# One layer of a diffusion backbone: order of the transposed pieces, a key load kept, and five buffers in two sizes

## The chip, the cores and the metric

The kernel runs on 1 core of one Trainium2 chip. The metric is the device time of one execution in microseconds (us); lower is better. All arithmetic of the layer is on the core; the host only supplies two rotary tables.

## The reference, cut to what matters

One trunk layer over 2048 latent tokens and 256 context tokens, width 1024. A combined projection feeds two attention mixers whose queries are the 2048 latent tokens and whose keys are all 2304 tokens; both results are gated, projected, merged and normalised. What bears on the change is the pair of attentions and how the first one's key is made:

```python
k_mla = concatenate([k_nope, broadcast_to(k_r, ...)])      # 8 heads, 64 + 32 columns; k_r is one for all heads
s = einsum('bhqd,bhkd->bhqk', q, k) * scale
o_a = einsum('bhqk,bhkd->bhqd', softmax(s), v)             # 8 heads

s1, s2 = (q1 k1, q2 k2) * scale                            # 4 heads, 64 columns each
p = softmax(s1) - lam * softmax(s2)
o_d = einsum('bhqk,bhkd->bhqd', p, v)
```

The first is called MLA below (kind 0 in the code), the second differential attention (kind 1).

## The kernel before, in words

Three stages follow each other: projections (to about 945 us), attention (to about 2530 us), and the output stage. Values that must be exact to fp32 are kept as a high and a low part, and a product is two or three matmuls.

**Attention.** Work comes in units of 256 queries of one head, two tiles of 128 queries each. There are 64 MLA units (8 heads of 8) and 32 differential ones (4 heads of 8); the order repeats two MLA units and one differential unit, 32 times, with a differential unit ahead. For each tile `softmax_tile` (L673) makes scores on TensorE in three PSUM groups (L682), VectorE takes each out with a running minimum (L683), ScalarE applies the exponential (L696). A differential tile does that twice, and VectorE combines the two (L795).

**`transposed` (L702)** turns a tile of 128 queries by 2304 keys around for the second product. The keys are 18 blocks of 128, in two halves of nine. For each half (e = 0, 1) ScalarE casts blocks to fp16 as a high part (L708), GpSimd subtracts to get the low part (L709, VectorE for some of the last units), and one transposing DMA on SyncE's queue (L710) moves both, turned, into `pts`. The buffer that holds the split, `hl`, comes from a pool of 4 equal buffers. A differential tile does so with 9 + 9 blocks. An MLA tile leaves 4 blocks of its first half out (5 + 9, `NCB` = 5): those four go through TensorE's transpose into the one PSUM buffer `px` (L715), from which ScalarE writes the high part (L717) and VectorE the low part (L718). In the source these four come after both casts.

**The second product** (`mla_av`, `diff_av`, L723 to L757) reads `pts`, has four tiles of `pt` (two units' worth) and runs on TensorE among the scores. A filler on TensorE (L627, gate projections, `pf`) is strewn between.

**Loads.** `load_k` (L799) fetches a head's keys when its first unit comes: three groups of 1024, 768 and 512 keys, each with its own buffer. For MLA, rows 0 to 63 (`kn`) are the head's own, rows 64 to 95 (`kr`) the rotary rows, which are the same for all heads. Both are loaded for each head; after the third unit the loads are issued on ScalarE's queue. MLA heads change seven times, the first at about 1098 us.

**Order.** Source order gives priorities; a planner works out each engine's fixed order when the kernel is built, putting a later instruction ahead where an earlier one is not yet ready by its plan. Every engine then works in that order.

Of the kernel before, what the change touches and what calls it, by code (L numbers as in the profile page):

```python
# [10 lines left out]
F32R = mybir.dt.float32r  # L11
F16 = mybir.dt.float16
I32 = mybir.dt.int32
AF = mybir.ActivationFunctionType
ALU = mybir.AluOpType
# [3 lines left out]
P = 128  # L19
# [44 lines left out]
def layer_kernel(ctx: ExitStack, tc: tile.TileContext, x, c, ctxt, c_ctx, w_mod, b_mod, w_in,  # L64
# [3 lines left out]
    pe, dve, act, pool, sp = nc.tensor, nc.vector, nc.scalar, nc.gpsimd, nc.sync  # L68
# [9 lines left out]
    def dram(name, shape, dt):  # L78
        return dr.tile(shape, dt, tag=name, name=name)
# [7 lines left out]
    kr_s = dram("kr", [32, 2, NT], F32)  # L87
# [502 lines left out]
    with ExitStack() as st:  # L590
        kp, qp_, vp = {}, {}, {}
# [11 lines left out]
        p16 = st.enter_context(tc.tile_pool(name="c16", bufs=4))  # L603
# [12 lines left out]
        def ldma(o, i):  # L616
            lq[0].dma_start(o.bitcast(F32) if o.dtype == F32R else o, i.bitcast(F32) if i.dtype == F32R else i)
# [81 lines left out]
        def new_pts():  # L699
            return [ptp.tile([P, 9, 2, 2, P], F16, tag="pt", name="pt") for _ in range(2)]  # L700

        def transposed(pts, i, s, shared, ncb):  # L702


            for e, n in enumerate((ncb, 9)):
                hl = p16.tile([P, 9, 2, P], F16, tag="hl", name="hl")[:, :n]
                se = s[:, e * 1152:e * 1152 + n * P].rearrange("p (k q) -> p k q", q=P)
                act.copy(hl[:, :, 0], se)  # L708
                (dve if shared and e else pool).tensor_tensor(hl[:, :, 1], se, hl[:, :, 0], op=ALU.subtract)  # L709
                sp.dma_start_transpose(pts[e][:, :n, :, i, :].rearrange("p k l q -> p (k l) q"),  # L710
                                       hl.rearrange("p k l q -> p (k l q)"))
            for k0 in range(ncb, 9, 4):
                px = ps_x.tile([P, 4, P], F32, tag="px", name="px")
                for t in range(4):
                    pe.transpose(px[:, t, :], s[:, (k0 + t) * P:(k0 + t + 1) * P], ident)  # L715
                hi, lo = (pts[0][:, k0:k0 + 4, l, i, :] for l in range(2))
                act.copy(hi, px)  # L717
                dve.tensor_tensor(lo, px, hi, op=ALU.subtract)  # L718

        def pt_part(pts, kt, l):  # L720
            return pts[kt // 9][:, kt % 9, l].rearrange("p i q -> p (i q)")
# [49 lines left out]
        def mla_soft(h, u, qt, ks, pts):  # L771
            for i in range(2):
                qs = qt[0:96, :, i * P:(i + 1) * P]
                k_hi, k_lo = (lambda k: k[0:96, 0, :]), (lambda k: k[0:96, 1, :])
                s = softmax_tile([(qs[:, 0, :], k_hi), (qs[:, 0, :], k_lo), (qs[:, 1, :], k_hi)], ks, MLA_SCALE, LN_PSC,
                                 zs[u][:, i, h:h + 1])
                transposed(pts, i, s, n_ >= len(units) - 2, NCB)
                yield

        def diff_soft(h, u, qt, ks, pts):  # L780
            for i in range(2):
                def scores(m, shift, zsum):
                    qs = qt[:, m, :, i * P:(i + 1) * P]
                    km = (lambda k: k[:, m, :])
                    return softmax_tile([(qs[:, 0, :], km), (qs[:, 1, :], km)], ks, DIFF_SCALE, shift, zsum)


                za = zs[u][:, i, H + h:H + h + 1]
                sa = scores(0, lamc[:, 2:3], za)
                yield  # L790
                w = sm.tile([P, 3], F32, tag="w", name="w")
                sb = scores(1, None, w[:, 0:1])
                dve.reciprocal(w[:, 1:2], w[:, 0:1])
                dve.tensor_scalar(w[:, 2:3], za, w[:, 1:2], lamc[:, 0:1], op0=ALU.mult, op1=ALU.mult)
                dve.scalar_tensor_tensor(sa, sb, w[:, 2:3], sa, op0=ALU.mult, op1=ALU.add)  # L795
                transposed(pts, i, sa, n_ >= len(units) - 3, 9)
                yield

        def load_k(kind, h):  # L799
            ks = []  # L800
            for g, (k0, nk) in enumerate(GS):
                k = kp[kind].tile([P, 2, nk], F32R, tag=f"k{kind}{g}", name=f"k{kind}{g}")
                cs = slice(k0, k0 + nk)
                if kind == 0:
                    ldma(k[0:64], kn_s[h // 2][(h % 2) * 64:(h % 2) * 64 + 64, :, cs])
                    ldma(k[64:96], kr_s[:, :, cs])
                else:
                    ldma(k, dk_s[h][:, :, :, cs].rearrange("l d m n -> (l d) m n"))
                ks.append(k)
            return ks  # L810
# [31 lines left out]
        for n_ in range(len(units) + LAG):  # L842
# [3 lines left out]
            if n_ < len(units):  # L846
                kind, h, u = units[n_]
                if u == 0:
                    ks_[kind] = load_k(kind, h)
                if n_ + 1 < len(units):  # L850
                    qs_.append(load_q(*units[n_ + 1]))
                pts = new_pts()
                soft = (mla_soft if kind == 0 else diff_soft)(h, u, qs_.pop(0), ks_[kind], pts)
            parts = (2 if kind == 0 else 4)
            g = None
            if len(pend) == LAG or (soft is None and pend):
                g = pend.pop(0)(parts)
# [21 lines left out]
    with ExitStack() as st:  # L879
# [20 lines left out]
        with ExitStack() as s1_:  # L900
# [70 lines left out]
            for b in range(8):  # L971
                cs = slice(b * 256, (b + 1) * 256)
# [119 lines left out]
```

## Time and profile before

| | |
|---|---|
| median of 3 runs | 2961.67 us (2951.07 to 2964.77) |
| the profiled execution | 2959.4 us |
| its span, first to last instruction | 2957.3 us |
| busy share of the span | PE 93%, PEld 75%, DVE 60%, ACT 49%, POOL 51% |
| granted TensorE clock, mean | 0.974 |

PE is TensorE's matmuls, PEld its weight loads, DVE VectorE, ACT ScalarE, POOL GpSimd, SP SyncE. An engine's busy time counts execution, not waiting. In the listed waits, "A <- B: total, times, longest" says that A stood idle until B was done. L708 is line 708 of the kernel.

### The profile page before, as it was taken

The page shows a single profiled execution, that of the slowest core. Times are in us where ns is not written, and L with a number is a line of the kernel's source. Part 1 is how long each engine was busy: PE and PEld are TensorE (multiplying, and loading weights), DVE is VectorE, ACT ScalarE, POOL GpSimd, SP SyncE. Part 2 cuts the span into 40 slices and gives each one's busy share as a digit, 9 for nine tenths or more (in the row PEclk, how much of TensorE's full clock was granted, in tenths as well). Part 3 has the DMA queues.
Part 4 walks back from the last instruction along what each step waited for, and adds up shares of the span by engine and source line. Part 5 has one row for each costly group of instructions (what it writes and reads, how often), then busy time and mean ns, then how long its engine had stood idle before and what let it go on. Part 6 is the DMA issues. An engine that isn't in the chain of part 4 may idle for free. (4 is left out here: it accounts for less than half of the span.)

```text
span 2957.3 us, 44828 instructions
## 1 busy us (share of the span) xinstructions
PE 2743.9 (93%) x16049; PEld 2205.0 (75%) x16049; DVE 1789.1 (60%) x3663; ACT 1446.6 (49%) x1885; POOL 1518.7 (51%) x1018
## 2 busy tenths in 40 slices
PE   7999999999999999989999999899899978889998
PEld 5888888879777777767767677677666656789886
DVE  4476310033656777767777777667667778675454
ACT  3333222233324767767766677666676667322110
POOL 2443222232445657658556586565576545464344
PEclk9999999999999999999999999999999989899999
DMA  8467533354566999999999999999999999877542
GB/s 261 124 193 219 165 103 90 97 165 129 147 199 163 194 175 210 187 219 195 176 198 228 213 204 191 196 174 184 195 185 178 198 181 166 232 207 221 178 146 82
DMA packets 1138914, 529.99 MB, mean 179 GB/s; under 512 B 818858, under 2 KB 1090944, under 8 KB 1138692
## 3 DMA queue, kind: packets, MB, share of 16 engines
q1 hardware_dynamic: 1014984, 421.65, 65.0%
q10 hardware_dynamic: 123708, 105.49, 15.1%
q8 instruction: 126, 2.06, 0.3%
q14 instruction: 96, 0.79, 0.1%
HBM read 219.96 MB, written 114.10 MB: 113 GB/s over the span
## 5 line engine op out<-in xcount | busy, mean ns | idle before, releaser
L709 POOL TENSOR_TENSOR hl<-s,hl 128x1152 f16<-128x1152 f32 (+1 forms) x378 | 790.9, 2110 | 468.4 <-ACT hl L708 424.2
L682 PE MATMUL ps<-k,q 96*128 96x512 f32 (+3 forms) x3200 | 822.7, 390 | 44.0 <-DVE s L683 41.2
L682 PEld LDWEIGHTS ps<-k,q 96*128 96x128 f32 (+1 forms) x3200 | 545.1, 192 | 164.7 <-DVE s L683 62.3
L696 ACT ACTIVATE s<-s,z 128x2304 f32<-128x2304 f32 x256 | 567.5, 2217 | 71.6 <-DVE z L689 34.3
L708 ACT CAST hl<-s 128x1152 f16<-128x1152 f32 (+1 forms) x384 | 375.9, 1007 | 345.5 <-DMA pt<-hl 184.5
L683 DVE TENSOR_SCALAR_CACHE_REDUCE s<-ps,z 128x768 f32<-128x768 f32 (+1 forms) x512 | 449.9, 880 | 126.1 <-PE ps L682 107.5
L683 DVE TENSOR_SCALAR_CACHE_REDUCE s<-ps 128x1024 f32<-128x1024 f32 x256 | 312.2, 1219 | 110.6 <-PE ps L682 94.3
L114 PE MATMUL pp<-hT,w 128*128 128x512 f32 (+1 forms) x896 | 347.4, 390 | 9.4 <-DVE qa L337 6.9
L115 PE MATMUL pp<-hT,w 128*128 128x512 f32 (+1 forms) x896 | 348.4, 390 | 0.3 <-DVE hT L272 0.3
L110 POOL TENSOR_TENSOR w<-raw,w 128x512 fp32r<-128x512 f32 (+1 forms) x126 | 163.9, 1307 | 359.7 <-ACT w L107 343.3
L116 PE MATMUL pp<-hT,w 128*128 128x512 f32 (+1 forms) x896 | 346.5, 388 | 0.0
L732 PE MATMUL po<-pt,vd 128*128 128x256 f16 x1728 | 242.4, 280 | 33.1 <-DMA pt<-hl 31.3
L732 PEld LDWEIGHTS <-vd 128*128 128x128 f16 x1728 | 157.8, 100 | 105.9 <-issue 71.8
L114 PEld LDWEIGHTS pp<-hT,w 128*128 128x128 f32 x896 | 169.0, 189 | 47.1 <-DVE qa L337 4.5
L115 PEld LDWEIGHTS pp<-hT,w 128*128 128x128 f32 x896 | 169.6, 189 | 36.4 <-POOL hT L272 0.6
L116 PEld LDWEIGHTS pp<-hT,w 128*128 128x128 f32 x896 | 169.2, 189 | 36.0
L795 DVE SCALAR_TENSOR_TENSOR s<-s,w 128x2304 f32<-128x2304 f32 x64 | 187.1, 2923 | 0.2
L745 PE MATMUL po<-pt,va 128*128 128x256 f16 x1152 | 168.2, 284 | 14.2 <-DMA pt<-hl 14.1
L1026 PE MATMUL pz<-wz,yt 128*128 128x512 f32 x768 | 179.6, 396 | 0.8 <-DVE z L1029 0.8
L1026 PEld LDWEIGHTS pz<-wz,yt 128*128 128x128 f32 x768 | 144.3, 188 | 35.8 <-DVE z L1029 1.3
L718 DVE TENSOR_TENSOR pt<-px,pt 128x512 f16<-128x512 f32 x128 | 87.9, 687 | 128.1 <-ACT pt L717 125.0
L745 PEld LDWEIGHTS <-va 128*128 128x128 f16 x1152 | 103.2, 101 | 70.7 <-issue 47.6
(233 smaller groups left out, 4709.4 us busy)
## 6 DMA issues: line engine op xcount, KB each, us to landing
raw<-in_w_in_dram SPq DMA_DIRECT2D x122, 256.0 KB, 3.1
fraw<-in_w_in_dram ACTq DMA_DIRECT2D x79, 256.0 KB, 5.1
xt<-in_x_dram SPq DMA_DIRECT2D x32, 512.0 KB, 5.1
mg<-gt SPq DMA_DIRECT2D x64, 256.0 KB, 4.2
q<-dq ACTq DMA_DIRECT2D x60, 256.0 KB, 5.4
gt<-o SPq DMA_DIRECT2D x54, 256.0 KB, 2.0
gt<-fo ACTq DMA_DIRECT2D x42, 256.0 KB, 4.3
kn<-kst SPq DMA_DIRECT2D x36, 256.0 KB, 3.4
```

The lines of the kernel that those rows point to most:

```text
L114: pe.matmul(ps, wh, mh, start=first, stop=False)
L115: pe.matmul(ps, wh, ml, start=False, stop=False)
L116: pe.matmul(ps, wl, mh, start=False, stop=last)
L682: pe.matmul(ps[:, c0:c1], qa, ka[:, c0:c1], start=(i == 0), stop=(i == len(qk) - 1))
L683: dve.tensor_scalar(s[:, k0:k0 + nk], ps, -scale, 3e38 if g == 0 else z[:, g - 1:g], op0=ALU.mult, op1=ALU.min, accum_out=z[:, g:g + 1])
L696: mark[0] = act.activation(s, s, AF.Exp, bias=b, scale=-1.0, accum_out=zsum).ins
L708: act.copy(hl[:, :, 0], se)
L709: (dve if shared and e else pool).tensor_tensor(hl[:, :, 1], se, hl[:, :, 0], op=ALU.subtract)
L732: pe.matmul(po, vv[:, w, kt, :], pt_part(pts, kt, l), start=(kt == 0 and i == 0), stop=(kt == NKT - 1 and i == 2))
L745: pe.matmul(po, vv[:, kt, :], pt_part(pts, kt, 0), start=(kt == 0), stop=(kt == NKT - 1))
L795: dve.scalar_tensor_tensor(sa, sb, w[:, 2:3], sa, op0=ALU.mult, op1=ALU.add)
L1026: pe.matmul(pz[:, n, :], y[:, yy, k, :], wz[k][ww][:, n * 512:(n + 1) * 512], start=(k == 0 and i == 0), stop=(k == KT - 1 and i == 2))
```

## The change

The block of four array-transposed pieces moves ahead of the two casts within `transposed`. The four equal `hl` buffers become three of nine blocks and two of five blocks (18,432 bytes a partition become 18,944). `load_k` loads the rotary rows for MLA head 0 only, ahead of that head's own rows, and keeps the three key tiles for the later heads, which load their own 64 rows into them.

```diff
         def transposed(pts, i, s, shared, ncb):
-            for e, n in enumerate((ncb, 9)):
-                hl = p16.tile([P, 9, 2, P], F16, tag="hl", name="hl")[:, :n]
-                se = s[:, e * 1152:e * 1152 + n * P].rearrange("p (k q) -> p k q", q=P)
-                act.copy(hl[:, :, 0], se)
-                (dve if shared and e else pool).tensor_tensor(hl[:, :, 1], se, hl[:, :, 0], op=ALU.subtract)
-                sp.dma_start_transpose(pts[e][:, :n, :, i, :].rearrange("p k l q -> p (k l) q"),
-                                       hl.rearrange("p k l q -> p (k l q)"))
             for k0 in range(ncb, 9, 4):
                 px = ps_x.tile([P, 4, P], F32, tag="px", name="px")
                 for t in range(4):
...
                 act.copy(hi, px)
                 dve.tensor_tensor(lo, px, hi, op=ALU.subtract)
+            for e, n in enumerate((ncb, 9)):
+                hl = p16.tile([P, n, 2, P], F16, tag=f"hl{n}", name="hl", bufs=3 if n == 9 else 2)
+                se = s[:, e * 1152:e * 1152 + n * P].rearrange("p (k q) -> p k q", q=P)
+                act.copy(hl[:, :, 0], se)
+                (dve if shared and e else pool).tensor_tensor(hl[:, :, 1], se, hl[:, :, 0], op=ALU.subtract)
+                sp.dma_start_transpose(pts[e][:, :n, :, i, :].rearrange("p k l q -> p (k l) q"),
+                                       hl.rearrange("p k l q -> p (k l q)"))
...
+        k0s = []
         def load_k(kind, h):
             ks = []
             for g, (k0, nk) in enumerate(GS):
-                k = kp[kind].tile([P, 2, nk], F32R, tag=f"k{kind}{g}", name=f"k{kind}{g}")
+                if kind == 0 and h > 0:
+                    k = k0s[g]
+                else:
+                    k = kp[kind].tile([P, 2, nk], F32R, tag=f"k{kind}{g}", name=f"k{kind}{g}")
                 cs = slice(k0, k0 + nk)
                 if kind == 0:
+                    if h == 0:
+                        ldma(k[64:96], kr_s[:, :, cs])
+                        k0s.append(k)
                     ldma(k[0:64], kn_s[h // 2][(h % 2) * 64:(h % 2) * 64 + 64, :, cs])
-                    ldma(k[64:96], kr_s[:, :, cs])
```

## Rows read from the trace of the kernel before

**Rows 1.** Busy time by stretch, whole attention stage; instruction counts in brackets.
```profile
core 0: us, PE busy (x) PEld busy (x) DVE busy (x) ACT busy (x) POOL busy (x), PEclk, DMA share, GB/s
945.00:2530.00 1585.00, 1445.80 (x8696) 1093.97 (x8697) 1159.48 (x2439) 1088.42 (x1206) 996.35 (x545) 0.96 1.02 193
```

**Rows 2.** Waits of TensorE in that stage: us in total, times, longest.
```profile
PE ps L682 <- DVE s L683: 41.2, 37, 4.6
PE po L732 <- DMA pt<-hl: 31.3, 16, 9.2
PE po L750 <- DMA pt<-hl: 16.4, 3, 9.0
PE po L745 <- DMA pt<-hl: 14.1, 6, 5.0
PE px L715 <- DVE pt L718: 13.4, 10, 4.0
```

**Rows 3.** Waits of ScalarE and VectorE in that stage.
```profile
ACT hl L708 <- DMA pt<-hl: 184.5, 94, 10.1
...
ACT pt L717 <- PE px L715: 13.8, 8, 5.7
...
DVE pt L718 <- ACT pt L717: 125.0, 52, 9.8
```

**Rows 4.** Busy time by stretch: a quiet one, then the seven changes of MLA head.
```profile
1050.00:1098.00 48.00, 46.81 (x288) 36.28 (x286) 37.35 (x81) 31.85 (x34) 26.42 (x16) 1.00 0.95 178
1098.00:1116.00 18.00, 12.70 (x67) 9.64 (x66) 9.08 (x22) 8.12 (x10) 8.61 (x5) 0.81 1.05 209
1292.00:1320.00 28.00, 22.89 (x138) 17.48 (x138) 14.02 (x36) 15.98 (x20) 11.71 (x8) 0.88 1.14 181
1490.00:1516.00 26.00, 23.44 (x146) 17.39 (x145) 15.79 (x38) 18.46 (x22) 15.39 (x10) 1.00 1.15 236
1690.00:1716.00 26.00, 22.93 (x139) 17.10 (x138) 14.06 (x33) 15.00 (x18) 12.75 (x8) 0.93 1.17 215
1882.00:1908.00 26.00, 23.78 (x159) 18.58 (x158) 15.53 (x37) 16.71 (x20) 13.15 (x9) 1.00 1.16 216
2088.00:2114.00 26.00, 15.38 (x94) 11.74 (x94) 11.08 (x25) 15.42 (x16) 8.86 (x5) 0.87 1.13 198
2300.00:2326.00 26.00, 21.11 (x133) 15.88 (x132) 13.65 (x31) 13.88 (x17) 11.16 (x6) 1.00 1.15 189
```

**Rows 5.** DMA issues: times, size, median us from issue to landing.
```profile
k<-kn ACTq DMA_DIRECT2D x7, 512.0 KB, 7.0
...
k<-kn ACTq DMA_DIRECT2D x7, 384.0 KB, 7.6
...
k<-kr ACTq DMA_DIRECT2D x7, 256.0 KB, 8.2
...
k<-kr ACTq DMA_DIRECT2D x7, 192.0 KB, 13.8
```

**Rows 6.** Instructions in order of time: start, us, engine; idle time before in brackets.
```profile
1501.46 0.63 PE L715 MATMUL px<-ident,s 128*128 128x128 f32 x4 [1.46 <-DVE pt L718]
...
1511.00 0.58 ACT L717 CAST pt<-px 128x512 f16<-128x512 f32 x1
...
1511.62 0.69 DVE L718 TENSOR_TENSOR pt<-px,pt 128x512 f16<-128x512 f32 x1 [3.23 <-ACT pt L717]
...
1512.36 0.66 PE L715 MATMUL px<-ident,s 128*128 128x128 f32 x4 [0.75 <-DVE pt L718]
```

**Rows 7.** All that writes hl or turns it: ns min/median/max; then landing times.
```profile
L708 ACT CAST hl<-s x384: 707/1147/1166, 943.8 to 2519.3; 128x640 f16<-128x640 f32 x128, 128x1152 f16<-128x1152 f32 x64
...
L709 POOL TENSOR_TENSOR hl<-s,hl x378: 1392/2386/4715, 945.0 to 2522.5; 128x640 f16<-128x640 f32 x126, 128x1152 f16<-128x1152 f32 x63
...
DMA to landing us min/median/max: 3.4/5.7/19.1
```

**Rows 8.** DMA in the attention stage (volume), then 1400 to 1450 us in 40 slices.
```profile
DMA packets 890133, 305.64 MB, mean 193 GB/s; under 512 B 786006, under 2 KB 875222, under 8 KB 890006
...
DMA  7999999965096992999999999999900999999999
```

## The prediction

> **What bounds the kernel now.** I read the page first for the stages: all that the change touches lies in the attention stage, 945 to 2530 us, so I took the busy times of that stretch [rows 1]. TensorE is busy 1445.8 of 1585 us, every other engine under three quarters. So TensorE is nearest to being the bound, but not a wall: it stands idle for 139.2 us, and its granted clock is 0.96, between the levels of 1.2 and 2.4 GHz; at 0.04 below full that is another 0.04 x 1585 = 63.4 us of lost pace. Some 203 us are there to be won, if stalls go. Next come the waits of TensorE [rows 2]: it waits for score buffers that VectorE has not emptied (41.2), for turned probabilities that have not landed (31.3 + 16.4 + 14.1 = 61.8), and for `px` (13.4). Then those of the engines behind it [rows 3]: ScalarE stands 184.5 us, 94 times, with a cast in hand and no free `hl` buffer, because the transposing DMA that reads the buffer has not landed; VectorE stands 125.0 us in L718 because ScalarE has not yet done L717. These two hang together: the engines work in a fixed order, and while ScalarE is held at a cast, the `px` copy behind it is held, VectorE behind that, and the score buffers behind VectorE.
>
> The reader should see one such case [rows 6]: TensorE finishes four transposes at 1502.1 us (1501.46 + 0.63), ScalarE copies them out at 1511.0, VectorE follows at 1511.6 after 3.23 us of standing, and TensorE's next four transposes start at 1512.36, after a wait for the one `px` buffer.
>
> Last I cut out the seven changes of MLA head [rows 4]. In the quiet stretch TensorE is busy 46.81 of 48 us, 0.975. The seven stretches are 176 us long and hold 142.2 us of TensorE: 0.975 x 176 - 142.2 = 29.4 us of extra idling. Their clock, 0.81 to 1.00, costs 0.19 x 18 + 0.12 x 28 + 0.07 x 26 + 0.13 x 26 = 12.0 us more. The head changes cost 41.4 us together.
>
> **The change part by part.**
>
> *Rotary rows.* 21 loads go: seven each of 256, 192 and 128 KB, 576 KB a head beside the 1152 KB of `kn` that stay (512 + 384 + 256) [rows 5], so a third of the bytes of a head's key load. These loads land late: 8.2 us for 256 KB and 13.8 for 192 KB, against 7.0 and 7.6 for the larger `kn` loads issued just ahead. TensorE is not seen waiting for keys; what suffers is the transposing DMAs beside them, whose longest landing is 19.1 us against a median of 5.7 [rows 7]. By bytes a third of the 41.4 us goes, 13.8; by landing, where `kr` is the last to come, a half, 20.7. I take 15. Bounds: nothing, if the `kn` loads alone hold the transposes as long, and 41 if the stalls vanish. The write into a kept tile still waits for the old head's last scores, as the new tile did, and has the same work queued behind it; the 21 issues saved on ScalarE's queue ran beside its own work, and I cost them at nothing. Head 0 loads the same bytes in another order, while the first differential unit runs: nothing.
>
> *Array-transposed pieces first.* No instruction is added or removed; for 128 MLA tiles, four transposes, L717 and L718 get a higher priority than both casts, two subtractions and two transposing DMAs. Where the planner follows, L717 comes ahead of a cast that may stand for a buffer, so `px` and VectorE come free earlier. Directly that removes at most TensorE's 13.4 us for `px`; through VectorE it can reach into the 41.2 us for score buffers, 54.6 in all [rows 2]. I take the 13.4, say 13, because VectorE's other work explains the rest. In return the casts come later by one L717 (0.58 us, [rows 6]); GpSimd's subtraction and SyncE's DMA stand behind them, and after that the second product, which is planned units later; that slack hides it, and without it 128 x 0.58 = 74 us of ScalarE would be at stake. The new wait: ScalarE with L717 in front must wait until TensorE has done the four transposes. Today that is 8 waits, 13.8 us [rows 3]. I double it. A microsecond of ScalarE's standing costs TensorE about 61.8 / 184.5 = 0.33 us (its waits for turned data over ScalarE's waits for `hl`), so 13.8 more cost 5 us. Between nothing and all 128 tiles (128 x 1.7 = 218 us, 72 for TensorE) I stay near nothing, since the planner puts a ready cast ahead of a copy that isn't.
>
> *Five buffers.* A long split holds its buffer for at least 1.15 + 2.39 + 5.7 = 9.2 us (medians), a short one for 0.71 + 1.39 + 3.4 = 5.5 (minima) [rows 7]. Two MLA units and a differential one take 1585 / 32 = 49.5 us and make eight long splits and four short ones. Four shared buffers: (8 x 9.2 + 4 x 5.5) / 4 = 23.9 us of each buffer's 49.5. Afterwards three long ones: 8 x 9.2 / 3 = 24.5; two short ones: 11.0. So on average the long splits are no better off. What is won is in bursts: a differential tile's two casts and an MLA tile's two fill all four buffers today, and the next short cast stands; afterwards it has its own. At the head changes TensorE can have at most 29.4 of the 61.8 us, so at least 32.4 us of waiting for turned data lie elsewhere; I take a third, 11. Upper bound 32. Lower: a long cast that found the fourth buffer free now stands for the oldest of three; if each of 64 differential tiles stood once more for the mean wait (184.5 / 94 = 1.96 us), 125 us x 0.33 = 41 us would be lost.
>
> *Clock.* Outside the head changes the clock costs 63.4 - 12.0 = 51.4 us beside 139.2 - 29.4 = 109.8 us of idling, 0.47 us for each. The 13 + 11 - 5 = 19 us won there give back 9.
>
> Sum: 15 + 13 - 5 + 11 + 9 = 43 us. The profiled execution took 2959.4 us, 2.1 more than its span, which holds start and end. 2959.4 - 43 = 2916; the median of the runs stands 2.3 us above the profiled one, so 2918.
>
> **Rivals.**
>
> *The DMA engines are the wall.* Their share in the stage is 1.02 [rows 1]. Then buffers and order only lengthen each landing, and the bytes alone count: 7 x 576 KB = 4.13 MB of 305.64 [rows 8], 1.35% of 1585 us = 21 us, giving 2940. Against it: between 1400 and 1450 us three of 40 slices fall to 0 and four more below 7 [rows 8], so the engines run dry when nothing is handed to them. The Trainium skill, "DMA: Bandwidth & Descriptors", section "Issuing engines are not separate DMA queues", says that DMAs issued by different engines run on the same 16 and interleave; by that rule more transposes in flight beside ScalarE's loads would bring nothing, as in this rival. The late landings at the head changes agree with it, the empty slices say that the stage as a whole is not so.
>
> *ScalarE stands for the array.* With L717 in front, every MLA tile's casts wait until TensorE gets to the four transposes among scores and second products. Each waits 1.7 us as the eight do today: 218 us x 0.33 x 1.47 = 105 us, against 43 + 7 (the small new wait and its clock are in the sum) won, so 2962 + 55 = 3017. It decides from 50 / (0.33 x 1.47) = 103 us of such waits, 0.8 us a tile. At half the tiles it is 2965, at three quarters 2990. For it: TensorE is the busiest. Against it: only 8 waits today, and a ready cast may be planned ahead.
>
> *The change does not do what it says.* The planner keeps nearly the old order, since the copy isn't ready when the exponential ends and the casts are; the waits for long buffers stay, and the shorter head load is taken up by the `kn` loads. Then a few us are left: 2956.
>
> *The stalls feed each other.* Held casts hold everything, so freeing them frees VectorE and the scores as well: all 41 us at the head changes, half of 54.6 and 32.4 (43.5) with its clock (x 1.47 = 64): 2962 - 105 = 2857.
>
> **How the numbers follow.** Forecast (2900 to 2935) 0.46; DMA wall 0.15; ScalarE stands 0.12; no effect 0.15; stalls feed each other 0.12. About 0.5%, 15 us, is what a measurement of this kernel can tell from no change: below 2947 is faster, above 2976 slower. Faster: 0.46 + 0.12 + most of the wall (0.13) = 0.71. Slower: three quarters of the standing rival and a little for the long buffers, 0.11. Same: 0.18. The range leaves out the far half of the feeding rival and the slower part of the standing one: 2868 to 2968.
>
> **What would show it.** Right: 3 loads of `k` from `kr` instead of 24; the waits of ScalarE for `hl` well under 184.5, of VectorE in L718 well under 125.0; TensorE's waits for turned data and `px` shorter, the clock above 0.96; stretches at head changes with TensorE nearer to 0.975. Wrong: ScalarE's wait for `px` far above 13.8 (the standing rival), landings of transposes lengthening by what the waits lost (the wall), the same waits in the same places (no effect), or long casts standing behind three buffers. The order on all engines is planned anew, and a worse order elsewhere in the stage would upset the sum.

## The result and the profile after

The changed kernel takes 2929.05 us (median of 10 runs, 2916.42 to 2946.36), the one before 2961.93 (10 runs, 2945.42 to 2983.77): a ratio of 0.9894, 95% interval 0.9866 to 0.9922, so 31 us less (23 to 40). The forecast was 2918, 43 us less. The profiled execution took 2936.47 us, span 2934.7, 7 us above the median; single runs of either kernel spread by some 15 us to both sides, so one profile shows where time lies, and only the medians say how much of it there is.

Busy time by stretch, the kernel after: the attention stage, the quiet stretch, then 18, 28 and five times 26 us from each change of MLA head on, the lengths of [rows 4].

```profile
core 0: us, PE busy (x) PEld busy (x) DVE busy (x) ACT busy (x) POOL busy (x), PEclk, DMA share, GB/s
945.00:2510.00 1565.00, 1443.58 (x8770) 1101.05 (x8769) 1150.37 (x2442) 1090.19 (x1211) 991.83 (x543) 0.96 1.05 194
1050.00:1098.00 48.00, 48.00 (x294) 37.08 (x294) 36.59 (x80) 34.63 (x38) 28.89 (x16) 1.00 0.97 184
1104.00:1122.00 18.00, 17.32 (x115) 13.91 (x116) 11.89 (x29) 11.43 (x12) 10.19 (x7) 1.00 1.24 217
1295.00:1323.00 28.00, 24.23 (x157) 18.05 (x156) 16.67 (x40) 17.44 (x22) 16.90 (x12) 0.97 1.16 207
1482.00:1508.00 26.00, 17.55 (x110) 13.17 (x109) 11.65 (x26) 12.65 (x15) 12.74 (x7) 0.89 1.16 163
1700.00:1726.00 26.00, 20.14 (x135) 15.57 (x133) 14.33 (x33) 15.87 (x18) 12.87 (x8) 0.96 1.16 178
1897.00:1923.00 26.00, 17.75 (x98) 13.78 (x97) 13.16 (x32) 15.24 (x18) 14.19 (x9) 0.87 1.12 162
2090.00:2116.00 26.00, 20.09 (x117) 15.62 (x115) 15.53 (x38) 20.57 (x24) 17.75 (x12) 0.93 1.14 205
2278.00:2304.00 26.00, 20.84 (x126) 15.49 (x127) 12.24 (x28) 12.81 (x14) 12.43 (x7) 0.94 1.21 167
```

The head changes did not get better in this execution: TensorE is busy 17.32 + 24.23 + 17.55 + 20.14 + 17.75 + 20.09 + 20.84 = 137.9 of 176 us, against 142.2 in [rows 4]. What was won lies elsewhere, and a little is lost again at the end. The cleanest cut is where the output matrix's first matmul starts (`py`, the first product of the output stage; 2528 us before, 2497 after). Up to there, before:

```profile
945.00:2528.00 1583.00, 1443.80 (x8687) 1091.97 (x8688) 1159.48 (x2439) 1087.99 (x1206) 996.35 (x545) 0.96 1.02 193
```

and after:

```profile
945.00:2497.00 1552.00, 1431.90 (x8695) 1089.90 (x8693) 1137.61 (x2419) 1082.00 (x1194) 986.20 (x537) 0.97 1.05 193
```

The attention stage became 31 us shorter: TensorE's idling fell from 139.2 to 120.1 us, and the same matmuls took 1431.9 us instead of 1443.8, at a clock of 0.97 instead of 0.96. From there to the end it is 437.7 us instead of 429.3, so 8 us were given back in a stage that the diff does not touch. This pair of executions is thus 22.6 us apart, less than the medians.

The waits of the kernel after, engine by engine, in the attention stage (to 2500 us): TensorE's,

```profile
PE po L732 <- DMA pt<-hl: 25.5, 16, 6.0
PE ps L682 <- DVE s L683: 21.2, 18, 4.5
PE po L745 <- DMA pt<-hl: 18.6, 6, 5.9
PE px L708 <- DVE pt L711: 12.6, 5, 7.9
PE po L750 <- DMA pt<-hl: 11.9, 2, 6.0
```

ScalarE's,

```profile
ACT hl L715 <- DMA pt<-hl: 121.1, 56, 7.3
...
ACT pt L710 <- PE px L708: 30.0, 14, 5.5
```

and VectorE's.

```profile
DVE pt L711 <- ACT pt L710: 79.6, 43, 9.0
```

L708, L710 and L711 are the former L715, L717 and L718; L715 is now the cast. Against [rows 2] and [rows 3]: ScalarE's standing for `hl` fell from 184.5 to 121.1 us, VectorE's from 125.0 to 79.6, TensorE's for score buffers from 41.2 to 21.2, for turned data from 61.8 to 56.0. The wait for `px` stayed (13.4, now 12.6), and ScalarE's wait for TensorE's four transposes doubled (13.8, now 30.0).

The DMA view after, key loads, and the landing line of the tile `hl`:

```profile
k<-kn ACTq DMA_DIRECT2D x7, 512.0 KB, 6.9
...
k<-kn ACTq DMA_DIRECT2D x7, 384.0 KB, 11.6
...
k<-kn ACTq DMA_DIRECT2D x7, 256.0 KB, 13.9
```

```profile
DMA to landing us min/median/max: 3.4/5.3/19.6
```

The rotary loads are gone, but the last load of a head still lands 13.9 us after its issue, as late as the rotary load of 192 KB did before (13.8, [rows 5]); the longest landing of a transposing DMA is still above 19 us [rows 7], its median a little shorter.

### The profile page after: what moved, and what is told of

Same layout as the page of the kernel before. It is cut to its first block, busy times and chain, and to the rows that moved or that the text cites. A ratio compares the mean times of both kernels' runs of the same rounds, so it can differ in the third digit from the quotient of the medians.

```text
span 2934.7 us, 44740 instructions
## 1 busy us (share of the span) xinstructions
PE 2734.8 (93%) x16049; PEld 2203.5 (75%) x16049; DVE 1776.3 (61%) x3663; ACT 1448.3 (49%) x1885; POOL 1517.4 (52%) x1018
## 4 chain that ended last, share of the span: by engine, by line
PE 61%; DMA 16%; DVE 8%; issue 5%; POOL 4%; ACT 3%; SPq 2%; ACTq 0%; POOLq 0%; DVEq 0%
PE ps L682 13%; DMA pt<-hl 8%; PE pp L114 7%; PE pp L115 7%; PE pp L116 7%; PE pz L1034 6%; PE po L732 5%; PE po L745 3%; DVE s L683 2%; PE po L750 2%; POOL hl L716 2%; ACT s L696 2%; PE pf L114 2%; PE pf L115 1%; PE pf L116 1%
## 5 line engine op out<-in xcount | busy, mean ns | idle before, releaser
L716 POOL TENSOR_TENSOR hl<-s,hl 128x1152 f16<-128x1152 f32 (+1 forms) x378 | 776.9, 2077 | 381.0 <-ACT hl L715 349.9
L682 PE MATMUL ps<-k,q 96*128 96x512 f32 (+3 forms) x3200 | 823.3, 390 | 22.5 <-DVE s L683 22.3
L682 PEld LDWEIGHTS ps<-k,q 96*128 96x128 f32 (+1 forms) x3200 | 548.1, 193 | 137.3 <-DVE s L683 33.6
L715 ACT CAST hl<-s 128x1152 f16<-128x1152 f32 (+1 forms) x384 | 372.1, 1009 | 267.6 <-DMA pt<-hl 121.1
L110 POOL TENSOR_TENSOR fw<-fraw,fw 128x512 fp32r<-128x512 f32 x84 | 125.6, 1495 | 122.5 <-ACT fw L107 103.3
L795 DVE SCALAR_TENSOR_TENSOR s<-s,w 128x2304 f32<-128x2304 f32 x64 | 173.9, 2717 | 0.3
L745 PEld LDWEIGHTS <-va 128*128 128x128 f16 x1152 | 101.3, 100 | 73.7 <-issue 47.2
```

Source lines behind the costliest of these rows:

```text
L110: eng_lo.tensor_tensor(lo, t32, hi.bitcast(F32) if hi.dtype == F32R else hi, op=ALU.subtract)
L682: pe.matmul(ps[:, c0:c1], qa, ka[:, c0:c1], start=(i == 0), stop=(i == len(qk) - 1))
L745: pe.matmul(po, vv[:, kt, :], pt_part(pts, kt, 0), start=(kt == 0), stop=(kt == NKT - 1))
```

## The experiments

The three parts are called order (the array-transposed block ahead of the casts), buffers (three long, two short) and rotary (the rows loaded once). Each ratio is to the kernel before on the same chip, over several rounds of both.

### Each part alone

Order: the kernel before, with the block moved up, the four equal buffers and the loads for each head kept.

```diff
+            for k0 in range(ncb, 9, 4):
+                px = ps_x.tile([P, 4, P], F32, tag="px", name="px")
...
             for e, n in enumerate((ncb, 9)):
                 hl = p16.tile([P, 9, 2, P], F16, tag="hl", name="hl")[:, :n]
```

> The kernel before with the four array-transposed pieces ahead of the two casts, and nothing else. By my sum (13 won at px, 5 lost to the new wait, 4 of clock) it takes 12 us off: ratio 0.996, VectorE's standing in the low-part subtraction clearly under 125 us. If the DMA engines are the wall: 1.000, with ScalarE's wait for hl still near 185 us. If ScalarE stands for the array: slower, its wait for px far above 14 us. If what a planned order costs is chance (each edit plans all engines anew), the time may lie anywhere within 15 us of before and the three parts alone do not add up to the 33 us.

Measured 1.0001 [0.9973, 1.003].

Buffers: the kernel before, with one line changed.

```diff
-                hl = p16.tile([P, 9, 2, P], F16, tag="hl", name="hl")[:, :n]
+                hl = p16.tile([P, n, 2, P], F16, tag=f"hl{n}", name="hl", bufs=3 if n == 9 else 2)
```

> The kernel before with three long and two short split buffers, and nothing else. By my sum (11 won, 5 of clock) 16 us off: ratio 0.995, ScalarE's wait for hl well under 184.5 us. If the DMA engines are the wall: 1.000, with the landing of the transposing DMAs longer by what the wait lost. If the differential tiles' long casts now stand behind three buffers: slower by up to 40 us, ratio up to 1.014.

Measured 1.001 [0.9982, 1.0038].

Rotary: the kernel before, with the new `load_k`.

```diff
+                if kind == 0 and h > 0:
+                    k = k0s[g]
...
+                    if h == 0:
+                        ldma(k[64:96], kr_s[:, :, cs])
+                        k0s.append(k)
                     ldma(k[0:64], kn_s[h // 2][(h % 2) * 64:(h % 2) * 64 + 64, :, cs])
-                    ldma(k[64:96], kr_s[:, :, cs])
```

> The kernel before with the rotary rows loaded once, and nothing else. By my sum 15 us off: ratio 0.995, the seven head changes with less idling of TensorE than 29 us. If the DMA engines are the wall: 21 us off, 0.993, which is then nearly all of the gain of the whole change. If the remaining key loads hold the transposes as long: 1.000.

Measured 0.9969 [0.9945, 0.9992]: 9 us.

Taken singly the parts are worth 0, -3 and 9 us, 6 together, where all three bring 31. So they don't add up: the 25 us between the two are clear of the noise, some 18 us for such a sum of ratios. What the buffers were to do, they did: ScalarE's standing for `hl` fell to 101.3 us (54 times) with them alone. That did not reach the end.

### The loads that stay

The changed kernel, but heads 1 to 7 load nothing.

```diff
-                    ldma(k[0:64], kn_s[h // 2][(h % 2) * 64:(h % 2) * 64 + 64, :, cs])
+                    if h == 0:
+                        ldma(k[0:64], kn_s[h // 2][(h % 2) * 64:(h % 2) * 64 + 64, :, cs])
```

> The changed kernel, in which MLA heads 1 to 7 also leave out the load of their own 64 key rows (they score against the keys of head 0), so that an MLA head change loads no key at all. It prices what the head changes still cost. By my sum they cost 41 us before and 26 after: about 26 us under the changed kernel, ratio to before 0.980. If the head changes never mattered much and the gain came from order and buffers: within 8 us of the changed kernel, 0.987 to 0.990.

Measured 0.9754 [0.9721, 0.9788], so 1.4%, 41 us, below the changed kernel. ScalarE's standing for `hl` halves once more:

```profile
ACT hl L715 <- DMA pt<-hl: 61.3, 36, 5.6
```

The key loads that are still there cost as much as the prediction had given to all key loads of the kernel before. Seven times 1152 KB are 8.26 MB, which by the bytes alone, reckoned as in the rival of the DMA wall, would be 43 us; so this run can't tell whether the loads cost by their bytes or by what they hold up.

### Each part left out

The changed kernel without the order (both casts first again):

```diff
-            for k0 in range(ncb, 9, 4):
-                px = ps_x.tile([P, 4, P], F32, tag="px", name="px")
...
             for e, n in enumerate((ncb, 9)):
                 hl = p16.tile([P, n, 2, P], F16, tag=f"hl{n}", name="hl", bufs=3 if n == 9 else 2)
...
+            for k0 in range(ncb, 9, 4):
+                px = ps_x.tile([P, 4, P], F32, tag="px", name="px")
```

> The changed kernel with the casts first again (buffers and rotary rows as changed). The parts alone gave 1.000 (order), 1.001 (buffers) and 0.997 (rotary), so their sum is 6 to 9 us of the 31. If order and buffers help only together (a copy that is ahead of the casts and casts that need not stand): about 0.996 to 0.998, the gain of the rotary rows alone. If the order does nothing in any company: 0.989, the changed kernel's ratio.

Measured 0.9871 [0.984, 0.9902]: the whole gain without the order.

Without the buffers (four equal ones):

```diff
-                hl = p16.tile([P, n, 2, P], F16, tag=f"hl{n}", name="hl", bufs=3 if n == 9 else 2)
+                hl = p16.tile([P, 9, 2, P], F16, tag="hl", name="hl")[:, :n]
```

> The changed kernel with four equal split buffers again (order and rotary rows as changed). If order and buffers help only together: 0.996 to 0.998. If the buffers do nothing: 0.989. If rotary rows and order are the pair that matters: near 0.99 with ScalarE's wait for hl still near 180 us.

Measured 0.9926 [0.9901, 0.9952].

Without the rotary part (the old `load_k`):

```diff
-                    if h == 0:
-                        ldma(k[64:96], kr_s[:, :, cs])
-                        k0s.append(k)
                     ldma(k[0:64], kn_s[h // 2][(h % 2) * 64:(h % 2) * 64 + 64, :, cs])
+                    ldma(k[64:96], kr_s[:, :, cs])
```

> The changed kernel with the rotary rows loaded for each head again (order and buffers as changed). If the three parts simply add, as my sum has them: 0.992 to 0.994 (the changed kernel's 0.989 plus the 0.003 that the rotary rows give alone). If the head changes are the place of the gain and the rotary rows are worth more once the splits are not short of buffers: 0.997 to 1.000.

Measured 1.001 [0.9984, 1.0037]: nothing is left.

And the block between the casts, with `cast` the old loop body as a function:

```diff
+            cast(0, ncb)
             for k0 in range(ncb, 9, 4):
...
+            cast(1, 9)
```

> The changed kernel with the array-transposed pieces between the first cast and the second one, a third place for the same work. If the place of the copy matters by the wait that it stands behind: between the changed kernel (0.989) and the one with the casts first. If what counts is the chance of the planned order, it may land outside of those two, by up to 15 us either way.

Measured 0.9876 [0.9843, 0.9909], the same as with the block behind or ahead.

These numbers fit what the planner made of the order. In the kernel after, the copy out of `px` still runs behind both casts of its tile on ScalarE. Here the first line, the second cast of the second line and the copy in the last belong to one MLA tile:

```profile
1094.01 0.73 ACT L715 CAST hl<-s 128x640 f16<-128x640 f32 x1
...
1095.70 2.20 ACT L715 CAST hl<-s 128x1152 f16<-128x1152 f32 x2
...
1098.82 0.57 ACT L710 CAST pt<-px 128x512 f16<-128x512 f32 x1
```

Counted in the programs as built, the copy stands behind both casts in 112 of the 128 MLA tiles before, in 112 with the order alone, in 123 in the kernel after and in 125 without the order; ahead of both it stands in 1, 2, 0 and 0. Putting the block in front in the source hardly moved it. With the buffers alone, adding the order moves one of ScalarE's 2150 instructions (waits not counted), and the kernel with the block between the casts has, instruction for instruction, the same program as the one without the order. So its 0.9876 beside 0.9871 is a second measurement of one program. Only where both other parts are in place does the block in front give a clearly different plan (633 of ScalarE's 2129 instructions stand elsewhere), and the time is the same within the noise.

The worth of each part beside the others, from these ratios (1% is 29.6 us; differences of two ratios are good to about 12 us):

| part | alone | beside one other | beside both others |
|---|---|---|---|
| rotary | 9 us | 22 (order), 41 (buffers) | 34 |
| buffers | -3 | -3 (order), 29 (rotary) | 9 |
| order | 0 | 0 (buffers), 13 (rotary) | -7 |

The gain is that of the rotary rows and the buffers together. Since the order changes the programs so little, rows that differ by it alone are nearly repeats: the rotary rows without the new buffers are worth 9 and 22 us, 15 in the mean, and nothing in the table clearly shows a worth of the order. The 9 us for the buffers beside both others lie within the noise; the 29 us beside the rotary rows do not. A rival is that a new plan is faster or slower by chance. Against it, the two quite different plans that have both parts, the kernel after and the one without the order, take the same time within the noise. For the kernels with one part or none there is no clearly different second plan, so the rival is not excluded there.

The kernel without the order also shows what the head changes could be. Its first loads come at 1102, 1294, 1485, 1692, 1878, 2067 and 2254 us:

```profile
1102.00:1120.00 18.00, 18.00 (x119) 14.28 (x120) 11.65 (x27) 13.46 (x14) 11.15 (x6) 1.00 1.19 225
1294.00:1322.00 28.00, 26.53 (x173) 20.41 (x171) 19.34 (x40) 16.30 (x20) 18.72 (x12) 1.00 1.22 225
1485.00:1511.00 26.00, 20.55 (x132) 15.72 (x130) 12.56 (x28) 11.83 (x13) 11.76 (x7) 0.93 1.20 166
1692.00:1718.00 26.00, 26.00 (x167) 19.78 (x166) 19.94 (x41) 16.79 (x21) 16.22 (x10) 0.95 1.18 217
1878.00:1904.00 26.00, 25.51 (x169) 19.52 (x168) 18.98 (x42) 17.45 (x20) 13.02 (x8) 1.00 1.15 216
2067.00:2093.00 26.00, 26.00 (x173) 20.11 (x170) 18.92 (x42) 16.89 (x21) 17.34 (x11) 1.00 1.19 228
2254.00:2280.00 26.00, 19.87 (x120) 14.92 (x120) 14.06 (x32) 15.53 (x18) 11.21 (x6) 0.91 1.03 152
```

TensorE is busy 162.5 of 176 us there, with the same loads as the kernel after (137.9), and its wait for `px` is shorter:

```profile
PE px L715 <- DVE pt L718: 3.3, 3, 1.5
```

So the order put in front brought no shorter wait for `px`, and in this pair of executions the head changes are worse with it. In the medians of this pair the order's price is 7 us with an uncertainty above that, so a loss by it is not shown. The windows themselves are more than one execution's luck: cut in the same way, they hold 155.4 us in the kernel with the block between the casts, which is the same program, and 165.7 in the kernel without the order and with 6 statistics buffers (below), against 136 to 148 in the ten others that load every head's keys, the kernel before and the one after among them. So the plan without the order did get better at the head changes, and the one of the kernel after did not. In all their medians the two plans are 5 us apart, good to 9 (0.9871, 0.9876 and 0.9873 against 0.9894 and 0.9888).

### What the buffers give back at the end

Reading all traces for the end of attention gives two groups. The last score matmul (L682), the first load of an output weight (`rawe`), and what is left of the span after that last score matmul starts:

| kernel | last score | first weight load | left of the span |
|---|---|---|---|
| before | 2509.2 | 2375.6 | 448 |
| order alone | 2485.4 | 2358.5 | 449 |
| rotary alone | 2494.6 | 2329.3 | 451 |
| without buffers | 2493.2 | 2331.0 | 452 |
| buffers alone | 2488.4 | 2510.3 | 471 |
| without rotary | 2492.2 | 2514.3 | 471 |
| without order | 2448.6 | 2469.3 | 468 |
| between the casts | 2466.6 | 2487.0 | 467 |
| no own keys | 2414.6 | 2436.5 | 468 |
| after | 2465.8 | 2487.4 | 469 |

With the new buffers the output weights are loaded only when attention is over, and some 18 us more pass after the last score. That is not all lost: from the last score on, before,

```profile
2509.20:2957.30 448.10, 408.56 (x2625) 365.38 (x2623) 260.11 (x545) 87.11 (x166) 207.42 (x202) 0.97 0.60 178
```

and after,

```profile
2465.80:2934.70 468.90, 421.82 (x2676) 373.24 (x2674) 267.68 (x563) 94.44 (x178) 211.58 (x206) 0.96 0.60 177
```

TensorE is busy 13.3 of the 20.8 us longer, in part with matmuls that ran ahead of the last score before. Its idling in this stretch is 38 to 41 us in the kernels with early loads, those of the tests below included, and 46 to 55 in those with late ones, some 10 us apart. In the kernel after, TensorE's last matmuls of attention and the first of the output stage, in order of time:

```profile
2486.72 2.08 PE L745 MATMUL po<-pt,va 128*128 128x256 f16 x9 [5.85 <-DMA pt<-hl]
2488.72 2.13 PE L750 MATMUL po<-pt,va 128*64 128x256 f16 x18
2490.79 1.70 PE L745 MATMUL po<-pt,va 128*128 128x256 f16 x9
2497.20 1.19 PE L114 MATMUL py<-u,wo 128*128 128x256 f32 x4 [4.71 <-issue]
```

TensorE is done at 2492.5 and starts the output product at 2497.2. The weights' casts on ScalarE start at 2490.4, three us after the first load (before: 2476.2, with 52 us to spare). The tile `rawe`, the first eight loads from the first of the two weight matrices (first and last start), after:

```profile
L902 SPq DMA_DIRECT2D rawe<-in_w_oa_dram x8: 327/430/532, 2487.4 to 2495.5; - x8
```

and before:

```profile
L894 SPq DMA_DIRECT2D rawe<-in_w_oa_dram x8: 417/512/1178, 2375.6 to 2533.1; - x8
```

The cause offered itself in the program's own map of on-chip memory (bytes of a partition), since a buffer of a later stage may not be written while the one that shared its bytes is in use:

```
first raw-weight buffers of the output stage      184,928 to 201,312
last hl buffer, kernel before                  ends at 184,736
last hl buffer, kernels with the new buffers   ends at 185,248
```

The 512 bytes more push `hl` over the border. Four kernels test this. The first is the kernel before with nothing changed but a pool of small statistics, which moves `hl` up by 512 bytes, to end at 185,248:

```diff
-        sm = st.enter_context(tc.tile_pool(name="csm", bufs=12))
+        sm = st.enter_context(tc.tile_pool(name="csm", bufs=20))
```

> The kernel before with 20 instead of 12 small statistics buffers below the split buffers, which only moves the four split buffers up by 512 bytes, as the changed buffers' end moves. In the kernel before they end at byte 184,736 of a partition, 192 below the first weight buffer of the output stage (184,928); here they end at 185,248, inside it. If that overlap is what holds the output weights back in all kernels with the new buffers: the first eight weight loads start after the last split instead of some 130 us before the end of attention, the time from the last score matmul to the end grows from 447 to about 468 us, ratio 1.006 to 1.007. If the late weight loads come from the planner's dealing with the new buffers: 1.000 and early loads.

Measured 1.0047 [1.0021, 1.0073]: 14 us slower, with the weights loaded late, as its `rawe` line shows (its last score matmul starts at 2524.3, with 466 us left):

```profile
L894 SPq DMA_DIRECT2D rawe<-in_w_oa_dram x8: 328/422/710, 2542.8 to 2550.8; - x8
```

The other three have 6 statistics buffers instead of 12, so that with the new buffers `hl` ends at 184,864, below the border. The changed kernel so:

```diff
-        sm = st.enter_context(tc.tile_pool(name="csm", bufs=12))
+        sm = st.enter_context(tc.tile_pool(name="csm", bufs=6))
```

> The changed kernel with 6 instead of 12 small statistics buffers, which moves the split buffers 384 bytes down, so that they end at 184,864, below the first weight buffer of the output stage again. If the overlap holds the output weights back: the first eight weight loads early again, 447 to 451 us from the last score to the end, about 18 us off the changed kernel, ratio to before 0.983. If not: 0.989.

Measured 0.9888 [0.9849, 0.9926]. The weights come at 2341.1 again and 456 us are left after the last score, but the time is that of the kernel after.

The same line in the kernel without the order:

> The buffers and the rotary rows of the changed kernel with the casts first, as in the run without the order, and 6 small statistics buffers. If the overlap holds the output weights back: 0.987 less 0.006, 0.981, the fastest of all. If the order is worth something once the tail is mended: slower than the changed kernel with the same mending.

Measured 0.9873 [0.9848, 0.9899]: weights from 2294.4 on, 448 us left, and again no gain.

The same line in the kernel with the buffers alone:

> The kernel before with the three long and two short split buffers alone, and 6 small statistics buffers. Buffers alone gave 1.001. If they won about 20 us in attention and gave them back at the overlap: 0.994 here. If the buffers are worth nothing without the rotary rows: 1.000.

Measured 0.9975 [0.9949, 1.0]: weights from 2340.4 on, 456 us left. Beside 1.001 for the buffers alone that is 10 us, in the expected direction, though the two intervals overlap.

So that the overlap delays the loads is shown by seven kernels with it and seven without. What it is worth in the total is shown once by itself (14 us, the kernel before moved up) and leaned towards a second time. In the two kernels with all the gain, mending it brought nothing measurable: 2 us less and 1 us more, each good to some 13, so the 10 us of idling are not excluded there either. The windows show where the time lay without the order: from 945 us to the first output matmul, as it was,

```profile
945.00:2478.00 1533.00, 1429.47 (x8703) 1088.99 (x8702) 1146.35 (x2423) 1083.42 (x1194) 983.11 (x538) 0.97 1.05 196
```

and with 6 statistics buffers:

```profile
945.00:2489.00 1544.00, 1445.53 (x8704) 1096.91 (x8705) 1160.90 (x2451) 1091.89 (x1210) 989.63 (x547) 0.96 1.05 195
```

The same matmuls took 16 us longer at a granted clock of 0.96 instead of 0.97, while TensorE idled 5 us less (98.5 against 103.5). After that point 433 us are left instead of 439. The edit also plans the order anew, and these are single executions; more can't be said.

No kernel that loads every head's keys beats the kernel after by more than the intervals allow; the lowest is the one without the order, 0.9871.

## Why the prediction was right, and where its steps failed

The direction was right, and the size is in its range: 31 us (23 to 40) against 43. That the sum came so near is in part luck: the term for the order had nothing to show for it, and the rotary term was too small where all parts are together. Four of its steps did not go as it put them.

**Rotary rows (term 15).** Undersized: beside the other two parts they are worth 34 us, alone 9. The step that failed is the sizing by the seven windows, 41.4 us for all key loads and a third to a half of that for the rotary ones. The loads that remain cost 41 us by themselves (no own keys), so all together it is some 34 + 41 = 75 us. The windows are a poor measure of that: in the kernel after they did not improve at all, and in the plan without the order they did (155 to 166 us of TensorE against 142), yet the medians of the two plans don't differ beyond the noise. The half by landing was a poor guide too: the last load still lands after 13.9 us, only it is another one now.

**`px` first (13, less 5 for ScalarE's new wait).** Failed at its condition, "where the planner follows": the planner left the copy behind both casts in 123 of 128 tiles, so there was nothing to win and no new wait to pay. TensorE's wait for `px` did not go (12.6), and with the casts first and the other two parts in place it is 3.3. That ScalarE's wait doubled as foreseen (13.8 to 30.0 us) is luck: with the order alone it is 14.1. VectorE's standing behind the copy does fall, to 79.6, but it is 81.5 without the order. The order is worth nothing measurable here: -7 us, good to 12.

**Buffers (11).** Beside the other two parts they are worth 9 us, good to 12, which neither confirms nor refutes the 11; beside the rotary part alone 29, without it nothing. And the mechanism had a part that the step did not see. The change as described makes the buffers 512 bytes larger, and the prediction has no term for their place; with that place the output stage's first load comes 18 to 22 us behind the last score instead of 126 to 179 ahead of it, and in the kernel before that alone is worth 14 us. The feared long casts behind three buffers did not show: ScalarE waits for `hl` 56 times instead of 94.

**Clock (9).** About right: the same matmuls take 12 us less up to the first output matmul, beside 19 us less idling.

**The sum itself.** It added the parts as if each worked alone, and that failed most clearly: 6 us singly, 31 together. One link between buffers and loads can be read in the waits of SyncE's queue, on which all transposing DMAs are issued in order. Before, in the attention stage,

```profile
SPq L710 <- DMA k<-kn: 14.8, 4, 6.8
...
SPq L710 <- DMA k<-kr: 10.5, 2, 5.6
```

with the buffers alone,

```profile
SPq L710 <- DMA k<-kn: 45.5, 5, 14.3
...
SPq L710 <- DMA k<-kr: 5.5, 1, 5.5
```

and with both, without the order:

```profile
SPq L710 <- DMA k<-kn: 4.0, 1, 4.0
```

The queue of the transposes stands until a key load has landed, once for 14.3 us, and whatever is turned next waits with it. The programs as built show where the wait comes from: the loads and transposes of ScalarE's and SyncE's queues signal their landing on eight semaphores in turn, and a transpose whose semaphore was last given to a key load waits for that load, though it needs no key. Such a wait for `kn` or `kr` stands in front of 21 transposes before (11 of them for `kr`), of 22 with the buffers alone, 17 with the rotary part alone, 12 without the order and 15 in the kernel after. Over this stage such waits for `kn` and `kr` are 21.1 to 25.3 us in the three kernels with four buffers and all loads; 34.2 to 51.0 in the three with the new buffers and all loads; 11.3 and 3.8 with the rotary part and four buffers; none to 5.2 in the five with both that keep the heads' own loads. So with more buffers alone more of the transposes' time meets these loads, and with the rotary loads gone less does. What these waits are worth in the total was not tested, as no kernel gave the key loads semaphores of their own; it is a likely link between the two parts and not a shown one.

**The rivals.** *DMA engines the wall* (bytes alone, 21 us): refuted as it stood. The buffers, which change no byte, add 29 us to the rotary rows; the median landing fell from 5.7 to 5.3 us. But its price of a byte is not refuted: the rotary rows gave 9 to 41 us against its 21, and the loads that stay 41 against 43. The Trainium skill, "DMA: Bandwidth & Descriptors", section "Issuing engines are not separate DMA queues", says that DMAs issued by different engines run on the same 16 DMA engines and interleave. The late landing of a head's last key load, 13.9 us after and 8.2 without the order, fits that, but no run here separates it from other causes. *ScalarE stands for the array*: its wait is 30.0 us in 14 times, a seventh of the 218 that it needed; as the copy did not come to stand in front, the rival was hardly put to the test. *No effect*: refuted by the interval for the whole change, but right for the order, where the planner did keep nearly the old place, as this rival said. *Stalls feed each other* (2857): it had the right idea in that the parts work on one another, and the wrong size.

## What to carry to other kernels

Look in the planned order whether an edit of source order has arrived there at all, before pricing it. When several edits loosen the same knot, a sum of single terms is not their price: time them in pairs, since a part worth nothing alone (here the buffers) can be worth 29 us beside another. A pool that grows by a few hundred bytes can slide under a buffer of the next stage and hold its first loads back, so compare the memory map and the stretch behind the stage, not only the stage. Price a load that disturbs by leaving it out, not by the stall seen around its issue.

## What was not expected of the hardware

The queue that issues the transposing DMAs stood for key loads that another engine had issued: up to 14.3 us at once with the buffers alone, 25.3 us in total in the kernel before. That comes from the program, which shares eight semaphores among all these DMAs, and is seen in the trace only in the queue's own waits. And single executions of one program differ by some 1%: the kernel after ran from 2916.42 to 2946.36 us in ten runs, as much as the whole effect, so that only ratios over several rounds carry a verdict here.
